# Rotary tables, head norm weights, lambda vectors and most parameters of a transformer layer loaded after the last modulation chunk instead of before it

## The chip, the core and the metric

The kernel runs on one core of one Trainium2 chip. The metric is the device time in microseconds of one execution; of several runs the median counts. Five engines work side by side, each in its own fixed order: TensorE (PE in the profile, with PEld for its weight loads), VectorE (DVE), ScalarE (ACT), GpSimd (POOL) and SyncE (SP), which here only issues DMA transfers. An instruction waits until the semaphores it names have reached a value, and everything behind it on its engine waits with it.

## What is computed

One layer of a diffusion transformer on 256 latent tokens `x` and 256 context tokens, model width 2048. The part that the change touches is at the front: modulation columns, the normalised and modulated hidden tokens, and q and k with a norm over each head, a rotary turn by table, and a difference of two softmaxes weighted by lambda.

```python
lam = (jnp.exp(jnp.sum(lambda_q1[l] * lambda_k1[l]))
       - jnp.exp(jnp.sum(lambda_q2[l] * lambda_k2[l])) + lam_init)
mod = (jax.nn.silu(c) @ w_mod[l] + b_mod[l])[:, None, :]
sa, ca, ga, sm, cm, gm = jnp.split(mod, 6, axis=-1)
h = modulate(x, norm_attn_w[l], sa, ca)          # rmsnorm(x, w) * (1 + ca) + sa
p = h @ w_in[l]
q = axial_rope(rmsnorm(split_qk(p[..., Q_OFF:K_OFF]), q_norm_w[l]), row, col)
k = axial_rope(rmsnorm(split_qk(p[..., K_OFF:V_OFF]), k_norm_w[l]), row, col)
mix = token_mixer(q, k_all, v_all, ..., lam, lam_init, subln_w[l], pool_w[l], pool_scale[l], ...)
x = x + ga * mix
x = x + gm * sq_relu_mlp(modulate(x, norm_mlp_w[l], sm, cm), w_ff1[l], w_ff2[l])
```

`k_all` and `v_all` hold latent and context tokens; the context runs through the same norm, weights and a modulation of its own.

## The kernel before

**Tiling.** Weights stream from memory in chunks of 128 x 1024 fp32 (512 KB), issued by SP. A product is done in three matmuls on split operands: ACT copies the chunk's high part (`whi`), DVE subtracts it to get the low part (`wlo`). Both have three buffers, so a new `whi` waits until PE is done with the one three chunks back.

**Modulation stage.** The loop `for f in range(KT)` runs over 16 feature tiles. For each it loads four chunks of `w_m` (`mod_tile`, PE groups `mod`), turns the result (`blocks` on DVE, `modT` on PE) into columns (`col`), and makes 128 hidden features of both token sets (`features`: `hw`, `hL`, `hC` on DVE and ACT). Beside it the first halves of k (`w_k` banks: k0, k1 for latent tokens, k2, k3 for context) and q (`w_q` banks: q0, q1) are accumulated feature by feature (`product`), one chunk of `w_k` or `w_q` per tile. In this loop the order of PE, ACT and DVE is that of the code (`ordered`, `pin`).

**Parameters.** One tile `prm` of 128 x 325 holds the identity `ident` for transposes, `c`, biases, norm weights, pool scales, edge factors and the small matrix `stack`; SP loads it first of all, ahead of `xT` (L298). Rotary tables, head norm weights and lambda vectors lie in `in_prq` (640 columns); POOL issues their loads (L207), as entries `prq` of the load list behind the first `w_m` chunk of tiles 9 and 11. POOL has nothing else to do there, so the scheduler lets the first three go at the kernel's start and the fourth (`lq2`, `lk2`, into the same buffer) as soon as the first lambda sum is done. `tables(0)`, `tables(1)` and `tables(2)` follow the features of tiles 9, 11 and 13: the cosine and sine tables times the q norm weight (with 1/8), times the k norm weight, and lambda.

**Evacuation stage.** Behind the loop come `qk_evac` for k0 to k3, then q0 and q1. ACT copies a bank to `qraw` and squares it to `qsq`; DVE sums (`qss`), takes the root with ACT's logarithm and exponential (`rsq`: `rq_y`, `rq_t`), scales, and for k0, k1, q0, q1 multiplies by two tables; POOL adds both products; PE turns the result with `ident` (`qkT`), ACT copies it to `kT` or `qT`. The transposes are due a fixed number of weight chunks later (`later`, `tick`: 3, 4, 5, 6 chunks for k0 to k3, 6 and 7 for q0 and q1), while PE works on the eight chunks of `w_v`, part 0 (`v`). Working tiles (`work`) share nine buffers of 2 KB. Here the scheduler orders ACT and DVE. DVE also accumulates the gate modulation (`ga_bc`, L648 and L650) from chunks that are loaded and due between the others.

The instructions of the modulation loop all show line 68 in the profile (the `pin` helper).

Of the kernel before, what the change touches and what calls it, by code (L numbers as in the profile page):

```python
# [23 lines left out]
LAM0 = 0.8 - 0.6 * math.exp(0.0)
# [3 lines left out]
WINDOWS = (2, 4, 8, 16)  # L28


PRM = {}
_o = 0
for _n, _w in (("ident", 128), ("c", 16), ("cc", 16), ("bca", 16), ("bsa", 16), ("nw", 16), ("nmw", 16),
               ("pscale", 8), ("subln", 1), ("edge", 60), ("stack", 32)):
    PRM[_n] = (_o, _o + _w)
    _o += _w
PRM_W = _o

PRQ = {}
_o = 0  # L40
for _n, _w in (("cos", 128), ("sin", 128), ("wk", 64), ("wq", 64), ("lq1", 64), ("lk1", 64),
               ("lq2", 64), ("lk2", 64)):
    PRQ[_n] = (_o, _o + _w)
    _o += _w
# [4 lines left out]
def layer(ctx: ExitStack, tc, a, out):  # L49
    nc = tc.nc  # L50
# [4 lines left out]
    pin = tc.keep_in_program_order  # L55
# [19 lines left out]
    def work(name, shape=None, dt=F32):  # L75
        return pool.tile(shape or [P, 512], dt, tag="w2", name=name, bufs=9)
# [51 lines left out]
    def plan(name, *idx, rate=0.0):  # L128
        stream.append(((name,) + idx, rate))
# [3 lines left out]
    for f in range(KT):  # L133
        for i in range(4):
            plan("w_m", f, i)
            if i == 0 and f in (9, 11):
                plan("prq", f // 2 - 4)
        if f == 0:
            for i in range(4):
                plan("cT", i)  # L140
        if f % 2 == 0:
            plan("w_k", 0, f // 2)
        if f % 2 == 1 and f > 1 or f == 0:
            plan("w_q", 0, f // 2)
# [55 lines left out]
    def load_next():  # L200
        key, rate = stream[len(loaded)]
        src = a[key[0]]
        for i in key[1:] if key[0] != "prq" else ():
            src = src[i]
        if key[0] == "prq":
            for dst, names in prq[key[1]]:
                nc.gpsimd.dma_start(dst, a["prq"][:, PRQ[names[0]][0]:PRQ[names[-1]][1]])  # L207
            loaded.append((key, None, None))
            return
        if key[0] in ("cT", "x"):  # L210
            dst = cT[:, 4 * key[1]:4 * key[1] + 4, :] if key[0] == "cT" else x1_tile()[:, key[1], key[2] * 512:key[2] * 512 + 512]
            nc.sync.dma_start(dst, src)
            loaded.append((key, None, None))
            return
        n = src.shape[-1]
        if key[0] == "w_m":
            raw = mod_raw(*key[1:])
            sp.dma_start(raw, src)
            loaded.append((key, raw, raw))
            return  # L220
        if key[0] in ("w_k", "w_q") and key[1] == 0:
            raw = pool.tile([P, n], F32, tag="aT", name="raw", bufs=2)
            sp.dma_start(raw, src)
            loaded.append((key, raw, raw))
            return
        raw = raw_chunk(src, n)
        if key[:3] == ("w_ff2", 7, 3):
            r3 = raw.rearrange("p (k f) -> p k f", k=2)
            vec.tensor_mul(r3, r3, mods["gm"][:, 1536:2048].unsqueeze(1).broadcast_to([P, 2, 512]))
        if key == ("w_ff1a", 0):  # L230
            hi, lo = (pool.tile([P, n], F32R, tag="aT", name=nm, bufs=2) for nm in ("hi0", "lo0"))
        elif key == ("w_o", 3, 4):
            pair = s8("pair", [P, 2, 1024], F32R)
            hi, lo = pair[:, 0, :], pair[:, 1, :]
        elif key in (("w_ff1a", 2), ("w_ff1a", 3)):
            i = 2 * (key[1] - 2)
            if i == 0:
                early.append(s16("early", [P, 4, 1024], F32R))
            hi, lo = early[0][:, i, :], early[0][:, i + 1, :]
        elif key == ("w_ff1a", 1):  # L240
            halves = [[work(nm, dt=F32R) for nm in ("hi1", "lo1")] for _ in range(2)]
            for h in range(2):
                split(*halves[h], raw[:, h * 512:h * 512 + 512])
            loaded.append((key, *zip(*halves)))
            return
        else:
            hi = pool.tile([P, n], F32R, tag="whi", name="whi", bufs=3)
            lo = pool.tile([P, n], F32R, tag="wlo", name="wlo", bufs=3)
        act.copy(hi, raw)  # L249
# [44 lines left out]
        return y  # L294


    prm = pool.tile([P, PRM_W], F32, tag="prm", name="prm")
    nc.sync.dma_start(prm, a["prm"])  # L298
    xT = s16("xT", [P, KT, T])
    cT = s16("cT", [P, KT, T])  # L300
    for i in range(4):
# [32 lines left out]
    wkt = pool.tile([P, 64], F32, tag="wkt", name="wkt")
    wqt = pool.tile([P, 3, 64], F32, tag="wqt", name="wqt")
    prq = (((tabs[:, 2:4], ("cos", "sin")), (wkt, ("wk",)), (wqt, ("wq", "lq1", "lk1"))),
           ((wqt[:, 1:3], ("lq2", "lk2")),))
    lam2 = pool.tile([P, 2], F32, tag="lam2", name="lam2")
    nlam = lam2[:, 0:1]

    sub8 = pool.tile([P, 1], F32, tag="sub8", name="sub8")
    vec.tensor_scalar(sub8, pr("subln"), 1.0 - LAM0, None, ALU.mult)

    def lam_sum(i):
        lm = work("lm", [P, 64])
        vec.tensor_mul(lm, wqt[:, 1, :], wqt[:, 2, :])
        vec.reduce_sum(lam2[:, i:i + 1], lm, axis=AX.X)

    def tables(part):

        if part == 0:
            lam_sum(0)
            vec.tensor_scalar(wqt[:, 0, :], wqt[:, 0, :], 0.125, None, ALU.mult)
        if part < 2:
            wv = wkt if part else wqt[:, 0, :]
            for t in range(2):
                vec.tensor_mul(tabs[:, 2 * part, t, :], tabs[:, 2, t, :], wv)
                so = tabs[:, 2 * part + 1, t, :].rearrange("p (a b f) -> p a b f", a=2, b=2)
                si = tabs[:, 3, t, :].rearrange("p (a b f) -> p a b f", a=2, b=2)
                wr = wv.rearrange("p (a b f) -> p a b f", a=2, b=2)  # L360
                for b in range(2):
                    vec.tensor_mul(so[:, :, b, :], si[:, :, b, :], wr[:, :, 1 - b, :])
            return
        lam_sum(1)
        act.activation(lam2, lam2, AF.Exp)
        vec.tensor_sub(nlam, lam2[:, 1:2], nlam)
        vec.tensor_scalar(nlam, nlam, -LAM0, None, ALU.add)
# [191 lines left out]
    for f in range(KT):  # L559
# [28 lines left out]
        if f == KT - 1:  # L588
            product("kx", f - 1)
            features(f)  # L590
        if f % 2 == 1:
            keep("w_q", f // 2, first_chunk("w_q", 0, f // 2))
        for n in ("kx", "kc", "q") if 2 < f < KT - 1 else ("kc", "q") if f == 2 else ("kc",):
# [2 lines left out]
            keep("w_k", f // 2, first_chunk("w_k", 0, f // 2))  # L596
        if f < KT - 1:
            features(f)
        if f in (9, 11, 13):
            tables(f // 2 - 4)  # L600
    for n, k in (("kx", KT - 1), ("kc", KT - 1), ("q", KT - 2), ("q", KT - 1)):
        product(n, k)
    while len(loaded) < FIRST_LOADS + 2:
        load_next()
    ordered_pe[0] = ordered[0] = False
    kb, qb = fb["w_k"], fb["w_q"]
    qT = s8("qT", [P, NH, T])
# [212 lines left out]
    def pool_diff(g, w, ps, sums):  # L820

        d = work("d")
        n0, n1 = w // 2, w // 2 - 1
        e0 = PRM["edge"][0] + sum(x - 1 for x in WINDOWS[:g]) * 2
        for i, s in enumerate(sums):
            pin(vec.tensor_mul(s[:, 0:n0], s[:, 0:n0], prm[:, e0:e0 + n0]))
            if n1:
                pin(vec.tensor_mul(s[:, T - n1:T], s[:, T - n1:T], prm[:, e0 + n0:e0 + n0 + n1]))
            sl = slice(i * T, i * T + T)
            pin(vec.scalar_tensor_tensor(d[:, sl], s, 1.0 / w, ps[:, sl], ALU.mult, ALU.subtract))  # L830
        diff.append((work("dh", dt=F32R), work("dl", dt=F32R)))
        later(1, partial(split, *diff[-1], d))
# [380 lines left out]
```

## Time and profile before

| | |
|---|---|
| median of 3 runs | 1448.89 us (1448.64 to 1449.95) |
| profiled execution, its own time | 1449.65 us |
| its span, first to last instruction | 1447.9 us |
| mean granted clock of PE | 0.997 |
| VectorE busy | 984.4 us (68%) |
| ScalarE busy | 674.5 us (47%) |
| moved by DMA | 355.23 MB, mean 245 GB/s |

A page of the profile lists the busy time of each engine, the span in 40 slices, the DMA queues, the chain of work that ended last, and the costliest groups of instructions. Views of the trace give the rest: who waited for whom, the instructions of an engine in order of time, DMA issues with the time to landing, and busy time by windows. In a timeline row stand the start, the duration, the engine, the line, the operation, what it writes and reads, shapes, and in brackets how long the engine had been idle and what ended that. Consecutive equal instructions are one row, with their count.

### The profile page before, as it was taken

To read this page: it belongs to the slowest core of one execution; us is meant where nothing else is said; L and a number is where in the kernel's file an instruction comes from. 1 tells how busy PE (TensorE), PEld (TensorE's weight loads), DVE (VectorE), ACT (ScalarE), POOL (GpSimd) and SP (SyncE) were. 2 spreads that over 40 slices of the span, in tenths; PEclk is the share of its full clock that TensorE was granted. 3 is DMA by queue.
4 is the path that set the end of the run, shared out by engine and by line. 5 is a ranking of instruction groups with operands and counts; after the bars stand their busy time and mean duration, and the time that the engine had idled before them with its cause. 6 is when DMAs were issued, how large, how long until landed. Compare 5 with 4: busy or idle time off the path is not lost.

```text
span 1447.9 us, 19760 instructions
## 1 busy us (share of the span) xinstructions
PE 1430.3 (99%) x7448; PEld 1178.6 (81%) x7448; DVE 984.4 (68%) x1226; ACT 674.5 (47%) x901; POOL 171.4 (12%) x188
## 2 busy tenths in 40 slices
PE   6999999999999999999999999999999999999998
PEld 4667887788888888888878888888888888888887
DVE  4568785768888777787766665656657555555676
ACT  5235336466644444444535545445354453544432
POOL 1001110001520111110101100011000110000260
PEclk9999999999999999999999999999999999999999
DMA  9996683335699999999746776777766665565553
GB/s 378 409 407 249 216 315 118 97 127 168 194 304 323 357 325 338 333 357 334 226 160 208 239 242 229 252 231 255 251 228 241 216 204 189 190 201 187 191 195 127
DMA packets 100976, 355.23 MB, mean 245 GB/s; under 512 B 12864, under 2 KB 13520, under 8 KB 100880
## 3 DMA queue, kind: packets, MB, share of 16 engines
q1 hardware_dynamic: 96336, 344.93, 68.6%
q0 software_dynamic: 4256, 8.77, 2.7%
q8 instruction: 58, 0.95, 0.3%
q14 instruction: 38, 0.31, 0.1%
q10 hardware_dynamic: 288, 0.26, 0.1%
HBM read 347.61 MB, written 2.17 MB: 242 GB/s over the span
## 4 chain that ended last, share of the span: by engine, by line
PE 93%; DMA 5%; DVE 1%; ACT 0%; issue 0%; SPq 0%; DVEq 0%
PE f L1060 14%; PE f L460 8%; PE f L459 8%; PE f L465 8%; PE f L1062 7%; DMA raw<-in_w_m_dram 4%; PE pg L459 4%; PE pg L460 4%; PE pg L465 4%; PE pyy L460 2%; PE pyy L459 2%; PE v L460 2%; PE pyy L465 2%; PE v L459 2%; PE v L465 2%; PE wo L460 2%
## 5 line engine op out<-in xcount | busy, mean ns | idle before, releaser
L250 DVE TENSOR_TENSOR wlo<-raw,whi 128x1024 fp32r<-128x1024 f32 x428 | 527.7, 1243 | 288.5 <-ACT whi L249 190.9
L249 ACT CAST whi<-raw 128x1024 fp32r<-128x1024 f32 x428 | 447.9, 1047 | 513.5 <-PE f L460 184.0
L1060 PE MATMUL f<-h,whi 128*128 128x512 f32 x896 | 213.9, 391 | 0.0
L460 PE MATMUL f<-whi,act 128*128 128x512 f32 x512 | 199.4, 389 | 0.0
L459 PE MATMUL f<-whi,act 128*128 128x512 f32 x512 | 199.3, 389 | 0.0
L1060 PEld LDWEIGHTS f<-h,whi 128*128 128x128 f32 x896 | 165.1, 188 | 32.1
L465 PE MATMUL f<-wlo,act 128*128 128x512 f32 x512 | 136.9, 389 | 0.0
L1062 PEld LDWEIGHTS f<-h,wlo 128*128 128x128 f32 x896 | 114.9, 191 | 4.4
L1062 PE MATMUL f<-h,wlo 128*128 128x256 f32 x896 | 116.2, 283 | 0.0
L465 PEld LDWEIGHTS f<-wlo,act 128*128 128x128 f32 x512 | 96.1, 188 | 19.9
L460 PEld LDWEIGHTS f<-whi,act 128*128 128x128 f32 x512 | 96.2, 188 | 19.7
L459 PEld LDWEIGHTS f<-whi,act 128*128 128x128 f32 x512 | 96.2, 188 | 19.7
L459 PE MATMUL pg<-whi,hL 128*128 128x512 f32 x256 | 100.3, 392 | 0.0
L460 PE MATMUL pg<-whi,hL 128*128 128x512 f32 x256 | 99.7, 389 | 0.0
L1070 POOL TENSOR_TENSOR rsq<-relu 128x512 f32<-128x512 f32 x28 | 29.1, 1038 | 457.7 <-ACT relu L1069 447.5
L650 DVE SCALAR_TENSOR_TENSOR sb<-raw,sil,sb 128x1024 f32<-128x1024 f32 x60 | 76.8, 1280 | 0.0
L465 PE MATMUL pg<-wlo,hL 128*128 128x512 f32 x256 | 68.5, 389 | 0.0
L465 PEld LDWEIGHTS pg<-wlo,hL 128*128 128x128 f32 x256 | 48.1, 188 | 10.1
L459 PEld LDWEIGHTS pg<-whi,hL 128*128 128x128 f32 x256 | 48.1, 188 | 9.9
L460 PEld LDWEIGHTS pg<-whi,hL 128*128 128x128 f32 x256 | 48.1, 188 | 9.9
L277 DVE TENSOR_TENSOR act<-rsq,act 128x512 fp32r<-128x512 f32 x28 | 19.3, 690 | 53.3 <-ACT act L276 53.3
L1084 DVE TENSOR_TENSOR acc<-f,acc 128x512 f32<-128x512 f32 x48 | 30.9, 686 | 20.5 <-PE f L465 20.5
(288 smaller groups left out, 2189.5 us busy)
## 6 DMA issues: line engine op xcount, KB each, us to landing
raw<-in_w_ff_dram SPq DMA_DIRECT2D x240, 512.0 KB, 4.3
raw<-in_w_m_dram SPq DMA_DIRECT2D x64, 512.0 KB, 10.2
raw<-in_w_ga_dram SPq DMA_DIRECT2D x32, 512.0 KB, 4.2
raw<-in_w_gb_in_dram SPq DMA_DIRECT2D x32, 512.0 KB, 5.1
raw<-in_w_cm_dram SPq DMA_DIRECT2D x32, 512.0 KB, 5.6
raw<-in_w_ga_in_dram SPq DMA_DIRECT2D x32, 512.0 KB, 5.7
raw<-in_w_sm_dram SPq DMA_DIRECT2D x32, 512.0 KB, 5.6
raw<-in_w_o_dram SPq DMA_DIRECT2D x32, 512.0 KB, 5.4
```

The costliest lines, as they stand in the source:

```text
L249: act.copy(hi, raw)
L250: vec.tensor_sub(lo, raw, hi.bitcast(F32))
L277: vec.tensor_sub(lo, src, hi.bitcast(F32))
L459: pe.matmul(banks[t], tok(h, k, 0, tt), wt, start=k == 0, stop=False)
L460: pe.matmul(banks[t], tok(h, k, 1, tt), wt, start=False, stop=False)
L465: pe.matmul(banks[t], tok(h, k, 0, tt), wt, start=False, stop=k == 2 * nk - 1)
L650: pin(vec.scalar_tensor_tensor(o, raw, sil[:, 0, k:k + 1], o, ALU.mult, ALU.add))
L1060: pe.matmul(ps, hi[:, kk * P:kk * P + P], both(h2, k), start=k == 0, stop=False)
L1062: pe.matmul(ps[:, T:2 * T], los[k // 8][:, k % 8 * P:k % 8 * P + P], act_slice(h2, k, 0), start=False, stop=k == KT - 1)
L1070: gp.tensor_mul(sq, r, r)
L1084: vec.tensor_add(acc[:, t, gs], bs[t], acc[:, t, gs])
```

## The change

The layout of `prm` is changed so that what the start needs (112 of 325 columns) comes first; the other 213, with `ident`, `nmw`, `pscale`, `subln` and `edge`, go to a tile `prm_late`. The entries `prq` are gone from the load list. A new function `late_loads`, called right behind the features of tile 15, writes one column of each of four tiles on DVE and then has POOL load them: `wqk` (both head norm weights), `tabs` (cosine and sine), `prm_late`, and `lamv` (the four lambda vectors, in one of the nine working buffers). The write makes each load wait for that place. `tables(1)` now stands behind the loop, ahead of the k evacuations; `tables(0)` and `tables(2)` stand between the evacuations of k and of q, in the order of the code. `tables(0)` now overwrites the cosine and sine tiles.

```diff
-for _n, _w in (("ident", 128), ("c", 16), ("cc", 16), ("bca", 16), ("bsa", 16), ("nw", 16), ("nmw", 16),
-               ("pscale", 8), ("subln", 1), ("edge", 60), ("stack", 32)):
+for _n, _w in (("c", 16), ("cc", 16), ("bca", 16), ("bsa", 16), ("nw", 16), ("stack", 32), ("ident", 128), ("nmw", 16),
+               ("pscale", 8), ("subln", 1), ("edge", 60)):
...
+PRM_1 = PRM["ident"][0]
...
-            if i == 0 and f in (9, 11):
-                plan("prq", f // 2 - 4)
...
-        if key[0] == "prq":
-            for dst, names in prq[key[1]]:
-                nc.gpsimd.dma_start(dst, a["prq"][:, PRQ[names[0]][0]:PRQ[names[-1]][1]])
-            loaded.append((key, None, None))
-            return
...
-    prm = pool.tile([P, PRM_W], F32, tag="prm", name="prm")
-    nc.sync.dma_start(prm, a["prm"])
+    prm = pool.tile([P, PRM_1], F32, tag="prm", name="prm")
+    nc.sync.dma_start(prm, a["prm"][:, 0:PRM_1])
+    prm_late = pool.tile([P, PRM_W - PRM_1], F32, tag="prm_late", name="prm_late")
...
-    vec.tensor_scalar(sub8, pr("subln"), 1.0 - LAM0, None, ALU.mult)
+
+    def late_loads():
+
+        lamv.append(work("lamv", [P, 4, 64]))
+        for dst, src in ((wqk, a["prq"][:, PRQ["wq"][0]:PRQ["wk"][1]]), (tabs[:, 0:2], a["prq"][:, 0:PRQ["sin"][1]]),
+                         (prm_late, a["prm"][:, PRM_1:PRM_W]),
+                         (lamv[0], a["prq"][:, PRQ["lq1"][0]:PRQ["lk2"][1]])):
+            flat = dst if len(dst.shape) == 2 else dst[:, 0, :] if len(dst.shape) == 3 else dst[:, 0, 0, :]
+            vec.memset(flat[:, 0:1], 0.0)
+            nc.gpsimd.dma_start(dst, src)
...
-        lam_sum(1)
+        vec.tensor_scalar(sub8, pr("subln"), 1.0 - LAM0, None, ALU.mult)
+        for i in range(2):
+            lam_sum(i)
         act.activation(lam2, lam2, AF.Exp)
...
         if f == KT - 1:
             product("kx", f - 1)
             features(f)
+            late_loads()
...
-        if f in (9, 11, 13):
-            tables(f // 2 - 4)
...
     while len(loaded) < FIRST_LOADS + 2:
         load_next()
+    tables(1)
...
     for t in range(4):
         qk_evac(kb[t], t, 0, kT, 2, 3 + t)
+    ordered[0] = True
+    tables(0)
+    tables(2)
+    ordered[0] = False
     for t in range(2):
         qk_evac(qb[t], t, 0, qT, 0, 6 + t)
```

The order of PE and of SP is the same in both programs. On POOL the four loads of `in_prq` ahead of and behind the eight rows of biases (`row`) are gone, and the four late loads stand behind them.

On DVE, at the end of the modulation loop (from `hw` of tile 15 on), there stood:

```order
L68 SCALAR_TENSOR_TENSOR hw<-xT,col,rms 128x256
L68 SCALAR_TENSOR_TENSOR hw<-cT,col,rms 128x256
L68 SCALAR_TENSOR_TENSOR hL_727<-hw,col,hL_727 128x256
L68 SCALAR_TENSOR_TENSOR hC_728<-hw,col,hC_728 128x256
L68 TENSOR_TENSOR wlo<-raw,whi 128x1024 x3
L477 TENSOR_REDUCE qss<-qsq 128x8
```

Now there stands, from the last two rows of the features on:

```order
L69 SCALAR_TENSOR_TENSOR hL_725<-hw,col,hL_725 128x256
L69 SCALAR_TENSOR_TENSOR hC_726<-hw,col,hC_726 128x256
L69 MEMSET wqk 128x1
L69 MEMSET tabs 128x1
L69 MEMSET prm_late 128x1
L69 MEMSET lamv 128x1
L69 TENSOR_TENSOR wlo<-raw,whi 128x1024 x3
L69 TENSOR_TENSOR tabs<-tabs,wqk 128x64
L69 TENSOR_TENSOR tabs<-tabs,wqk 128x2x16 x2
L69 TENSOR_TENSOR tabs<-tabs,wqk 128x64
L69 TENSOR_TENSOR tabs<-tabs,wqk 128x2x16 x2
L481 TENSOR_REDUCE qss<-qsq 128x8
```

The six products of `tables(1)`, which need two of the loads, have come between the last `wlo` of the loop and the first sum for k0.

Further down on DVE, around the last table product for q0 (`qraw_1313<-qraw_1313,tabs_86`; q1 is `qraw_1333`), there stood:

```order
L650 SCALAR_TENSOR_TENSOR ga_bc_1353<-raw_1429,sil_80,ga_bc_1353 128x1024
L480 TENSOR_TENSOR qraw_1313<-qraw_1313,rq_y_1319 128x512
L292 SCALAR_TENSOR_TENSOR rq_t_1342<-qss_1337,rq_t_1342 128x8
L250 TENSOR_TENSOR wlo_1465<-raw_1462,whi_1464 128x1024
L487 TENSOR_TENSOR qsq_1315<-qraw_1313,tabs_86 128x8x16 x4
L293 SCALAR_TENSOR_TENSOR rq_y_1339<-rq_t_1342,rq_y_1339 128x8
L650 SCALAR_TENSOR_TENSOR ga_bc_1353<-raw_1468,sil_80,ga_bc_1353 128x1024
L489 TENSOR_TENSOR qraw_1313<-qraw_1313,tabs_86 128x512
L480 TENSOR_TENSOR qraw_1333<-qraw_1333,rq_y_1339 128x512
L487 TENSOR_TENSOR qsq_1335<-qraw_1333,tabs_86 128x8x16 x4
L250 TENSOR_TENSOR wlo_1504<-raw_1501,whi_1503 128x1024
```

Now q0 is `qraw_1318` and q1 `qraw_1338`:

```order
L244 TENSOR_TENSOR wlo_1509<-raw_1506,whi_1508 128x1024
L287 SCALAR_TENSOR_TENSOR rq_y_1324<-rq_t_1327,rq_y_1324 128x8
L285 SCALAR_TENSOR_TENSOR rq_t_1347<-rq_y_1344 128x8
L658 SCALAR_TENSOR_TENSOR ga_bc_1358<-raw_1512,sil_81,ga_bc_1358 128x1024
L484 TENSOR_TENSOR qraw_1318<-qraw_1318,rq_y_1324 128x512
L286 SCALAR_TENSOR_TENSOR rq_t_1347<-qss_1342,rq_t_1347 128x8
L491 TENSOR_TENSOR qsq_1320<-qraw_1318,tabs_87 128x8x16 x4
L287 SCALAR_TENSOR_TENSOR rq_y_1344<-rq_t_1347,rq_y_1344 128x8
L493 TENSOR_TENSOR qraw_1318<-qraw_1318,tabs_87 128x512
L484 TENSOR_TENSOR qraw_1338<-qraw_1338,rq_y_1344 128x512
L491 TENSOR_TENSOR qsq_1340<-qraw_1338,tabs_87 128x8x16 x4
L244 TENSOR_TENSOR wlo_1548<-raw_1545,whi_1547 128x1024
```

The `wlo` of the seventh `w_v` chunk (`wlo_1504` before, `wlo_1509` now) and the `ga_bc` step of its neighbour stand ahead of q0's last product now, where they stood behind it.

On ACT, around q0's root (`rq_y_1319` before: logarithm, then exponential):

```order
L249 CAST whi_1425<-raw_1423 128x1024
L288 ACTIVATE rq_y_1319<-qss_1317,epsb_73 128x8
L498 COPY kT_1242<-qkT_1431 128x4x128
L289 ACTIVATE rq_y_1319<-rq_y_1319,ebias_71 128x8
L288 ACTIVATE rq_y_1339<-qss_1337,epsb_73 128x8
L289 ACTIVATE rq_y_1339<-rq_y_1339,ebias_71 128x8
L249 CAST whi_1464<-raw_1462 128x1024
```

And now (`rq_y_1324`):

```order
L477 COPY qraw_1318<-w_q_0_242 128x512
L479 ACTIVATE qsq_1320<-w_q_0_242 128x512
L477 COPY qraw_1338<-w_q_1_243 128x512
L479 ACTIVATE qsq_1340<-w_q_1_243 128x512
L69 ACTIVATE lam2_89<-lam2_89 128x2
L282 ACTIVATE rq_y_1324<-qss_1322,epsb_74 128x8
L243 CAST whi_1508<-raw_1506 128x1024
L283 ACTIVATE rq_y_1324<-rq_y_1324,ebias_72 128x8
L282 ACTIVATE rq_y_1344<-qss_1342,epsb_74 128x8
```

Between the two halves of q0's root stands the `whi` cast of the seventh `w_v` chunk instead of a copy of `kT`, and lambda's exponential has come ahead of them.

More of the change, by code (lines that the diff above doesn't have):

```diff
@@ L37 @@
 PRM_W = _o
+PRM_1 = PRM["ident"][0]
 PRQ = {}
 _o = 0
-for _n, _w in (("cos", 128), ("sin", 128), ("wk", 64), ("wq", 64), ("lq1", 64), ("lk1", 64),
+for _n, _w in (("cos", 128), ("sin", 128), ("wq", 64), ("wk", 64), ("lq1", 64), ("lk1", 64),
                ("lq2", 64), ("lk2", 64)):
@@ L202, in load_next @@
         src = a[key[0]]
-        for i in key[1:] if key[0] != "prq" else ():
+        for i in key[1:]:
             src = src[i]
-        if key[0] == "prq":
-            for dst, names in prq[key[1]]:
-                nc.gpsimd.dma_start(dst, a["prq"][:, PRQ[names[0]][0]:PRQ[names[-1]][1]])
-            loaded.append((key, None, None))
-            return
         if key[0] in ("cT", "x"):
@@ L305, in pr @@
         lo, hi = PRM[name]
-        return prm[:, lo:hi]
+        return prm[:, lo:hi] if hi <= PRM_1 else prm_late[:, lo - PRM_1:hi - PRM_1]
     ident = pr("ident")
@@ L333, in layer @@
     tabs = pool.tile([P, 4, 2, 64], F32, tag="tabs", name="tabs")
[L334 to L337, printed above, removed]
+    wqk = pool.tile([P, 2, 64], F32, tag="wqk", name="wqk")
+    wkt = wqk[:, 1, :]
+    lamv = []
     lam2 = pool.tile([P, 2], F32, tag="lam2", name="lam2")
@@ L341, in layer @@
     sub8 = pool.tile([P, 1], F32, tag="sub8", name="sub8")
-    vec.tensor_scalar(sub8, pr("subln"), 1.0 - LAM0, None, ALU.mult)
+    def late_loads():
[6 more added lines that the diff above has]
+            nc.gpsimd.dma_start(dst, src)
     def lam_sum(i):
         lm = work("lm", [P, 64])
-        vec.tensor_mul(lm, wqt[:, 1, :], wqt[:, 2, :])
+        vec.tensor_mul(lm, lamv[0][:, 2 * i, :], lamv[0][:, 2 * i + 1, :])
         vec.reduce_sum(lam2[:, i:i + 1], lm, axis=AX.X)
     def tables(part):
-        if part == 0:
-            lam_sum(0)
-            vec.tensor_scalar(wqt[:, 0, :], wqt[:, 0, :], 0.125, None, ALU.mult)
         if part < 2:
-            wv = wkt if part else wqt[:, 0, :]
+            wv = wqk[:, part, :]
+            if part == 0:
+                vec.tensor_scalar(wv, wv, 0.125, None, ALU.mult)
             for t in range(2):
-                vec.tensor_mul(tabs[:, 2 * part, t, :], tabs[:, 2, t, :], wv)
+                vec.tensor_mul(tabs[:, 2 * part, t, :], tabs[:, 0, t, :], wv)
                 so = tabs[:, 2 * part + 1, t, :].rearrange("p (a b f) -> p a b f", a=2, b=2)
-                si = tabs[:, 3, t, :].rearrange("p (a b f) -> p a b f", a=2, b=2)
+                si = tabs[:, 1, t, :].rearrange("p (a b f) -> p a b f", a=2, b=2)
                 wr = wv.rearrange("p (a b f) -> p a b f", a=2, b=2)
@@ L823, in pool_diff @@
         n0, n1 = w // 2, w // 2 - 1
-        e0 = PRM["edge"][0] + sum(x - 1 for x in WINDOWS[:g]) * 2
+        e0 = sum(x - 1 for x in WINDOWS[:g]) * 2
         for i, s in enumerate(sums):
-            pin(vec.tensor_mul(s[:, 0:n0], s[:, 0:n0], prm[:, e0:e0 + n0]))
+            pin(vec.tensor_mul(s[:, 0:n0], s[:, 0:n0], pr("edge")[:, e0:e0 + n0]))
             if n1:
-                pin(vec.tensor_mul(s[:, T - n1:T], s[:, T - n1:T], prm[:, e0 + n0:e0 + n0 + n1]))
+                pin(vec.tensor_mul(s[:, T - n1:T], s[:, T - n1:T], pr("edge")[:, e0 + n0:e0 + n0 + n1]))
             sl = slice(i * T, i * T + T)
```

## The prediction

> **What bounds the kernel now.** The page comes first: busy times by engine.
>
> ```profile
> span 1447.9 us, 19760 instructions
> ## 1 busy us (share of the span) xinstructions
> PE 1430.3 (99%) x7448; PEld 1178.6 (81%) x7448; DVE 984.4 (68%) x1226; ACT 674.5 (47%) x901; POOL 171.4 (12%) x188
> ```
>
> TensorE (PE) is idle for 1447.9 - 1430.3 = 17.6 us in all, so nothing can be won but part of that, and every new wait of PE is lost time unless a later wait swallows it. The waits view of PE says where the idle time is, first for 0 to 130 us, then for the rest (columns: total us, times, longest).
>
> ```profile
> PE ssq L68 <- DVE sq L68: 9.4, 2, 7.7
> PE w_k L68 <- ACT hL L68: 1.6, 1, 1.6
> PE mod L68 <- DMA raw<-in_w_m_dram: 0.8, 3, 0.4
> ```
>
> ```profile
> PE qkT L497 <- ACT e L718: 0.5, 1, 0.5
> PE pd L281 <- DVE dl L277: 0.5, 1, 0.5
> ```
>
> Almost all of it lies in the first 35 us. Behind 130 us only 1.0 us is left, so a stall there has next to nothing to disappear into. The windows view gives the stages (columns: length, busy us and instructions of PE, PEld, DVE, ACT, POOL, then granted clock, DMA share, GB/s).
>
> ```profile
> 40.00:60.00 20.00, 20.00 (x197) 13.39 (x199) 11.60 (x26) 5.55 (x9) 0.00 (x0) 1.00 1.03 408
> ...
> 120.00:140.00 20.00, 19.99 (x96) 15.85 (x95) 17.29 (x39) 14.35 (x28) 2.77 (x2) 1.00 0.58 202
> 140.00:160.00 20.00, 20.00 (x97) 16.63 (x96) 19.96 (x34) 6.77 (x12) 6.00 (x3) 1.00 0.55 175
> ```
>
> Two stages matter. In the modulation stage (to about 120 us, one stretch of it is shown) the DMA queues are full (share 1.03, 408 GB/s) and PE is full too, while VectorE (DVE) has eight us in twenty to spare. From 120 to 160 us it is the reverse: the queues are half empty and DVE is full, 19.96 us of 20. The change takes bytes and DVE work out of the first stage and puts both into the second.
>
> **What the first stage gains.** Removed ahead of the last modulation chunk are 213 columns of `prm` (213 x 128 x 4 = 0.109 MB) and the 640 columns loaded from `in_prq` (0.328 MB). At 408 GB/s the 0.437 MB are worth 1.07 us. Small rows cost more than their bytes. The DMA view of 0 to 20 us, and then that of 84 to 96 us for the last of these loads, give the share of the 16 engines that the POOL queue took:
>
> ```profile
> q0 software_dynamic: 384, 0.30, 5.0%
> ```
>
> ```profile
> q0 software_dynamic: 32, 0.07, 1.5%
> ```
>
> 5.0% of 20 us is 1.0 us, 1.5% of 12 us is 0.18 us, and `prm` is 0.109/408 = 0.27 us: 1.45 us is the upper end. That PE gets all of it isn't given, since PE is itself gapless from 40 us on. PE wins by two ways: `xT` lands earlier, so the first squares and all that hangs on them move up, and its three waits for `w_m`, 0.8 us together, shrink. I put the first way at the 0.26 + 0.11 MB that left the queues before the last `xT`, 0.37/0.408 = 0.9 us, less some share that PE doesn't pass on. Ends: 0.6 and 1.45; I take **1.1 us gained**, the value of the plain bytes. The DVE work taken out there (20 table, lambda and `sub8` instructions) wins nothing: DVE waits for PE in every step of that stage.
>
> **What the second stage pays.** Now follow DVE. Its timeline before, around the end of the last features:
>
> ```profile
> 122.73 0.48 DVE L68 SCALAR_TENSOR_TENSOR hC<-hw,col,hC 128x256 fp32r<-128x256 f32 x1
> 123.67 3.50 DVE L68 TENSOR_TENSOR wlo<-raw,whi 128x1024 fp32r<-128x1024 f32 x3 [0.45 <-ACT whi L68]
> 127.08 0.68 DVE L477 TENSOR_REDUCE qss<-qsq 128x8 f32<-128x512 f32 x1
> 128.86 0.17 DVE L291 SCALAR_TENSOR_TENSOR rq_t<-rq_y 128x8 f32<-128x8 f32 x1 [1.10 <-ACT rq_y L289]
> ```
>
> From 127.08 to 160 us the only idle time is the 1.10 us shown. The POOL additions for k0, k1 and q0 (the rotary sums), and of the transposes on PE that take their results those for k0 and q0, are these:
>
> ```profile
> 133.00 2.20 POOL L490 TENSOR_TENSOR qraw<-qraw,qsq 128x512 f32<-128x512 f32 x1 [44.92 <-DVE rq_t L292]
> 139.43 1.65 POOL L490 TENSOR_TENSOR qraw<-qraw,qsq 128x512 f32<-128x512 f32 x1 [4.22 <-DVE qraw L489]
> 152.11 1.61 POOL L490 TENSOR_TENSOR qraw<-qraw,qsq 128x512 f32<-128x512 f32 x1 [11.04 <-DVE qraw L489]
> ```
>
> ```profile
> 138.90 0.60 PE L497 MATMUL qkT<-prm,qraw 128*128 128x128 f32 x4
> ...
> 156.61 1.04 PE L497 MATMUL qkT<-prm,qraw 128*128 128x128 f32 x8
> ```
>
> The x8 are four for k3 and four for q0. q0's begin about 1.04 - 0.60 = 0.44 us in, near 157.05 us, and its sum was there at 152.11 + 1.61 = 153.72 us: **3.3 us of slack**. k0's was there at 135.20 for 138.90: 3.7 us. PE's order is unchanged, so these are the places where it would wait.
>
> Step 1, the late loads. The four memsets stand behind hC, end 123.21 us, where DVE idled 0.45 us before `wlo`, and a memset of that size took 0.06 us in the run's first us (the first row below), so they are free. They release the loads on POOL. What such a load took, from the DMA view (KB, us from issue to landing), between the longest and the shortest POOL transfer:
>
> ```profile
> 0.82 0.06 DVE L312 MEMSET epsb<- 128x1 f32 x1
> ```
>
> ```profile
> ga_bc<-row POOLq DMA_DIRECT2D x2, 512.0 KB, 7.8
> ...
> tabs<-in_prq_dram POOLq DMA_DIRECT2D x1, 128.0 KB, 5.2
> ...
> gm_bc<-gm_bc POOLq DMA_DIRECT2D x2, 32.0 KB, 3.1
> ```
>
> `wqk` is issued at 123.3, `tabs` some 0.55 us later, at 123.85. With 5.2 us, the row of the same tile, `tabs` lands at 129.05; the bounds are 126.95 and 131.65. `tables(1)` waits for it, and in DVE's order everything of the k and q evacuations stands behind it, as do the low parts of the next `w_v` chunks. DVE was free at 127.08, so it starts **1.97 us late** (0 to 4.6). POOL holds nothing behind the loads but the k0 sum; the parameters with `ident` land two issues later, near 130.2, long before the transposes at 138.90.
>
> Step 2, work that comes ahead of q0's sum on DVE. The pieces, as they ran before:
>
> ```profile
> 87.00 0.22 DVE L68 TENSOR_TENSOR lm<-wqt 128x64 f32<-128x64 f32 x1
> 87.25 0.22 DVE L68 TENSOR_REDUCE lam<-lm 128x1 f32<-128x64 f32 x1
> 87.39 0.18 DVE L68 TENSOR_SCALAR wqt<-wqt 128x64 f32<-128x64 f32 x1
> 87.60 0.77 DVE L68 TENSOR_TENSOR tabs<-tabs,wqt 128x64 f32<-128x64 f32 x6
> 88.29 0.44 DVE L68 STREAM_TRANSPOSE blocks<-mod 128x256 f32<-128x256 f32 x1
> ```
>
> ```profile
> 156.14 1.27 DVE L650 SCALAR_TENSOR_TENSOR ga_bc<-raw,sil,ga_bc 128x1024 f32<-128x1024 f32 x1
> ```
>
> From start to start, six table products hold DVE 0.69 us (87.60 to 88.29), with the scaling 0.90; a lambda sum 0.39 (87.00 to 87.39). So: `tables(1)` 0.69, `tables(0)` 0.90, two lambda sums and the two operations that end lambda 1.0, `sub8` 0.1. And by the order one more `wlo` (three took from 123.67 to 127.08, 1.1 each) and one more `ga_bc` (1.27, 1.2 with the same overlap) now stand ahead of q0's last product, five and four where there were four and three. Together **5.0 us**.
>
> Step 3, a new wait of DVE. On ScalarE q0's logarithm and exponential now have a `whi` cast between them, as the ACT rows show; before, q0's root was ready when DVE came for it.
>
> ```profile
> 149.09 1.05 ACT L249 CAST whi<-raw 128x1024 fp32r<-128x1024 f32 x1 [2.69 <-PE v L460]
> ```
>
> The same pair, with a shorter square between, made DVE wait 1.10 us for k0 (above). With 1.05 us between, and 0.3 us of lambda operations for DVE to do meanwhile, I take **1.3 us**; the ends are 0, if other rows fill it, and 1.10 + 1.05 = 2.15.
>
> Sum for q0: 1.97 + 5.0 + 1.3 = 8.3 us later against 3.3 us of slack, a stall of **5.0 us** on PE near 157 us. The gain doesn't reduce it: PE and DVE both come 1.1 us earlier. With the landing at its late bound it is 7.6, with step 3 at its upper end too 8.5; with the early bound and without step 3 it is 5.0 - 3.3 = 1.7. For k0, ahead of its sum stand 1.97, 0.69 and one `wlo` more, 3.9 us against 3.7 of slack: next to no stall, and one in the late case. q1, whose transposes come a whole weight chunk behind q0's, gains the length of the stall and stays covered. Step 4 is the clock.
>
> ```profile
> 15.00:20.00 5.00, 2.40 (x28) 0.99 (x20) 3.84 (x9) 2.94 (x7) 0.00 (x0) 0.97 1.03 415
> 20.00:25.00 5.00, 5.00 (x16) 3.92 (x16) 3.68 (x6) 4.54 (x7) 0.00 (x0) 0.69 1.03 409
> ```
>
> PE idled 2.6 us of five, and its clock was lowered behind that: (0.03 + 0.31) x 5 = 1.7 us of full-speed time lost. A stall of 5 us should bring this on again, part of it while PE is still idle: **1.2 us** (0 to 1.7). The Trainium skill, "TensorE: Matmul & The Clock Gate", Part 1, says that the clock is halved after an idle window of about 3.4 us, in windows that run freely. This trace shows it after 2.6 us in pieces already, so 5 us should do by either.
>
> **The sum.** -1.1 + 5.0 + 1.2 = +5.1 us. On the profiled execution's 1449.65 us that is 1454.75; that execution lies 0.76 us over the median of the runs, 1448.89, so a median of **1454.0 us** is forecast, 0.35% slower. Bounds, from the median: -1.45 + 1.7 + 0 gives 1449.1; -0.6 + 8.5 + 1.7 gives 1458.5.
>
> **The rivals.**
> - *The stall doesn't come.* If the loads land before 126.95 us and DVE gets at q0's rows without the new wait, 5.0 us of work meets 3.3 us of slack, and another 1.7 us found (in DVE's 1.10 us of idle time and in its waits for the POOL sums, which fall elsewhere in the new order) hides all. Left is the gain: 1447.8 us. It decides when DVE's delay falls under 3.3 us. For it speaks that DVE has just 17.29 us of work from 120 to 140; against it, the 19.96 of the next 20 and the fixed order. Chance 0.16.
> - *The loads land early,* in 3.1 us like the quickest POOL row, so that `tables(1)` never waits: the stall is 1.97 us shorter, 1448.89 - 1.1 + 3.0 + 1.2 = 1452.0. For it: the queues are emptying when the loads are issued, and were full for the 5.2 us; against it: most POOL rows are nearer to 5 us than to 3. Chance 0.12. The Trainium skill, "DMA: Bandwidth & Descriptors", section "Anatomy of one DMA — SWDGE (gpsimd) path", speaks for this one: it fits such a load as 2.0 us plus bytes over 436 GB/s, an estimate of 2.3 us for `tabs`, where the row has 5.2.
> - *The loads land late,* 7.8 us after issue: k0's transpose stalls too and the PE total is 7.6: 1448.89 - 1.1 + 7.6 + 1.2 = 1456.6. For it: four loads are issued in a row; against it: the queues are half empty there. Chance 0.08.
> - *No stall, and the start loses its low-clock stretch,* because PE's early gaps move: -1.1 - 1.7 gives 1446.1. Chance 0.06.
>
> That the loads aren't held back at all isn't likely: POOL's rows wait for DVE.
>
> **How the numbers follow.** The forecast itself has 0.58. A measurement of this kernel can tell about 0.2%, 2.9 us, from no change. Of the 0.58, 0.04 lies under 1451.8 (no lowered clock, step 3 filled), of the early landing half, 0.06. So slower 0.54 + 0.06 + 0.08 = 0.68, within 0.2% 0.04 + 0.06 + 0.16 = 0.26, faster 0.06. The range is that of the bounds, 1449.1 to 1458.5; what it leaves out is the case without any stall, 0.16, and the one with the better start, most of whose 0.06 is under it.
>
> **What would show it.** In the profile after: PE's waits should have a row of `qkT` waiting for POOL's `qraw`, near 5 us in one piece, and no other new row; DVE should idle some 2 us ahead of the first `tabs` products; the waits for `w_m` should shrink from 0.8 us and the last `mod` matmuls come about 1.1 us earlier; the granted clock should dip in the stretch behind 160 us. It is wrong if `tabs` lands within 3 us of issue, if q0's transposes start without a wait, or if the `mod` matmuls end no earlier.

## The result, and the profile after

| | before | after |
|---|---|---|
| median | 1450.13 us, 12 runs | 1453.14 us, 12 runs |
| profiled execution, its own time | 1449.65 us | 1453.45 us |
| its span | 1447.9 us | 1451.6 us |

The changed kernel takes 1.0018 times as long, with a 95% interval of 1.001 to 1.0026: 2.6 us, from 1.5 to 3.8. One of the 12 runs of before took 1782.6 us; it is in the median but not in the ratio, and without it the median of before is 1449.95 us. The medians of the table lie 3.0 us apart. Note that the median of before lies 1.2 us over that of the three runs the prediction started from.

The page of the changed kernel, its first lines: PE is idle for 1451.6 - 1432.1 = 19.5 us, 1.9 more than before, while its busy time grew by 1.8, though it does the same 7448 matmuls. So the loss has two halves: waits, and matmuls that ran slower.

```profile
span 1451.6 us, 19767 instructions
...
PE 1432.1 (99%) x7448; PEld 1179.4 (81%) x7448; DVE 982.9 (68%) x1230; ACT 675.7 (47%) x901; POOL 170.0 (12%) x188
```

PE's waits after (total us, times, longest). New are the second row, the wait for q0's sum, and the fourth; the row for `w_m` is gone.

```profile
PE ssq L69 <- DVE sq L69: 8.4, 2, 6.7
PE qkT L501 <- POOL qraw L494: 2.8, 1, 2.8
PE w_k L69 <- ACT hL L69: 1.6, 1, 1.6
PE pg L463 <- ACT whi L243: 1.0, 1, 1.0
```

The timeline of PE after, at the first `w_v` matmul and at the transposes of k3 and q0. Before, `v` began at 128.01 and the transposes of k3 at 156.61: PE comes to both 1.9 us earlier, and then gives back 2.79 us in one piece.

```profile
126.04 0.39 PE L463 MATMUL v<-whi,hL 128*128 128x512 f32 x1
...
154.71 0.60 PE L501 MATMUL qkT<-prm_late,qraw 128*128 128x128 f32 x4
158.10 1.11 PE L501 MATMUL qkT<-prm_late,qraw 128*128 128x128 f32 x4 [2.79 <-POOL qraw L494]
```

The windows of that place (length, busy us of PE, PEld, DVE, ACT, POOL, granted clock, DMA share, GB/s). The clock falls to 0.78 and 0.88: (0.22 + 0.12) x 5 = 1.7 us of full-speed time. DVE, 19.96 of 20 before, is at 18.61 in the 20 us.

```profile
140.00:160.00 20.00, 17.21 (x81) 14.15 (x80) 18.61 (x47) 8.46 (x16) 1.89 (x2) 0.94 0.56 184
155.00:160.00 5.00, 2.21 (x10) 1.77 (x9) 4.96 (x12) 1.17 (x2) 1.58 (x1) 0.78 0.41 146
160.00:165.00 5.00, 5.00 (x21) 4.07 (x20) 1.73 (x2) 1.05 (x1) 2.17 (x1) 0.88 0.67 195
```

Upstream, DVE's timeline after shows the three things that came in ahead of q0: a wait for the table load, the tables and lambda, and a new wait for ScalarE at 150.74.

```profile
125.92 0.77 DVE L69 TENSOR_TENSOR tabs<-tabs,wqk 128x64 f32<-128x64 f32 x6 [0.70 <-DMA tabs<-in_prq_dram]
126.60 0.68 DVE L481 TENSOR_REDUCE qss<-qsq 128x8 f32<-128x512 f32 x1
128.32 0.17 DVE L285 SCALAR_TENSOR_TENSOR rq_t<-rq_y 128x8 f32<-128x8 f32 x1 [1.04 <-ACT rq_y L283]
...
139.07 1.27 DVE L285 SCALAR_TENSOR_TENSOR rq_t<-rq_y 128x8 f32<-128x8 f32 x1
...
144.73 0.19 DVE L69 TENSOR_SCALAR wqk<-wqk 128x64 f32<-128x64 f32 x1
144.95 0.77 DVE L69 TENSOR_TENSOR tabs<-tabs,wqk 128x64 f32<-128x64 f32 x6
...
150.74 0.17 DVE L285 SCALAR_TENSOR_TENSOR rq_t<-rq_y 128x8 f32<-128x8 f32 x1 [1.25 <-ACT rq_y L283]
...
155.63 0.69 DVE L493 TENSOR_TENSOR qraw<-qraw,tabs 128x512 f32<-128x512 f32 x1
```

POOL's sums for k0, k1 and q0 after. q0's ends at 156.47 + 1.58 = 158.05, where the transposes start. In relation to the start of `v` on PE that is 32.0 us; before it was 153.72 - 128.01 = 25.7. The sum is 6.3 us later, against the 3.3 us of slack.

```profile
133.49 1.28 POOL L494 TENSOR_TENSOR qraw<-qraw,qsq 128x512 f32<-128x512 f32 x1 [9.73 <-DVE rq_t L286]
138.72 1.59 POOL L494 TENSOR_TENSOR qraw<-qraw,qsq 128x512 f32<-128x512 f32 x1 [3.95 <-DVE qraw L493]
156.47 1.58 POOL L494 TENSOR_TENSOR qraw<-qraw,qsq 128x512 f32<-128x512 f32 x1 [16.15 <-DVE qraw L493]
```

The DMA view of 110 to 135 us after (KB, us from issue to landing): the late loads took 3.3 to 3.9 us.

```profile
tabs<-in_prq_dram POOLq DMA_DIRECT2D x1, 128.0 KB, 3.6
lamv<-in_prq_dram POOLq DMA_DIRECT2D x1, 128.0 KB, 3.3
prm_late<-in_prm_dram POOLq DMA_DIRECT2D x1, 106.5 KB, 3.4
wqk<-in_prq_dram POOLq DMA_DIRECT2D x1, 64.0 KB, 3.9
```

### The profile page after: what moved, and what is told of

It reads as the page before. It is cut to its first block, busy times and chain, and to the rows that moved or that the text cites. A ratio compares the mean times of both kernels' runs of the same rounds, so it can differ in the third digit from the quotient of the medians.

```text
span 1451.6 us, 19767 instructions
## 1 busy us (share of the span) xinstructions
PE 1432.1 (99%) x7448; PEld 1179.4 (81%) x7448; DVE 982.9 (68%) x1230; ACT 675.7 (47%) x901; POOL 170.0 (12%) x188
## 4 chain that ended last, share of the span: by engine, by line
PE 87%; issue 8%; DVE 2%; DMA 2%; ACT 1%; POOL 0%; DVEq 0%; ACTq 0%; POOLq 0%
PE f L1068 14%; PE f L464 8%; PE f L463 8%; PE f L469 8%; PE f L1070 7%; PE pg L463 4%; PE pg L464 4%; PE pg L469 4%; PE wo L463 2%; PE pyy L463 2%; PE pyy L464 2%; PE wo L469 2%; PE wo L464 2%; PE pyy L469 2%; PE v L463 1%
```

## The experiments

Theory: all that the change loses, it loses at q0's transposes, since DVE's rows ahead of q0's sum grew; the early loads it takes away are a gain. Rivals: the work has to be paid in any place; part of the loss lies elsewhere (a weight chunk near 505 us); the late landing or the late `ident` sets it. All edits are to the changed kernel unless said otherwise.

**Later q turns (e1).** The sums stay as late as they are; PE just doesn't ask for them yet.

```diff
-        qk_evac(qb[t], t, 0, qT, 0, 6 + t)
+        qk_evac(qb[t], t, 0, qT, 0, 7 + t)
```

> The transposes of q0 and q1 on PE stand one weight chunk later; DVE's order is that of the changed kernel. Theory A (the loss is PE's one wait for q0's POOL sum, 2.79 us, and the 1.7 us of lowered clock behind it): no wait of qkT for qraw, clock 1.00 from 155 to 165 us, and only the 1.9 us gained by 126 us is left: 1448.2 us where before has 1450.1, ratio 0.9987. Rival B (the work added to DVE between 125 and 160 us has to be paid, so the wait only moves, to the low parts of w_v or to q1): at least 1 us of PE waits in another row between 155 and 200 us, ratio 1.000 or over. Rival C (the 1.3 us that PE lost at a weight chunk near 505 us belong to the change too): no wait for qraw, but 0.9996, with a wait of pg for whi near 500 us.

Measured: 1448.81 us beside 1449.75 of before, ratio 0.999 (0.9981 to 0.9999). PE has no wait for `qraw`. Its windows show no idle time and a full clock where the changed kernel lost both, and DVE is as full as there:

```profile
155.00:160.00 5.00, 5.00 (x26) 4.12 (x25) 4.96 (x14) 1.15 (x2) 1.61 (x1) 1.00 0.49 179
160.00:165.00 5.00, 5.00 (x26) 4.12 (x25) 5.00 (x5) 1.08 (x2) 3.31 (x1) 1.00 0.58 179
```

The same work on DVE, in the same order, costs nothing once PE's demand stands one chunk later, so B falls. Between this kernel and the changed one lie 1.0018 - 0.999 = 0.0028, 4.1 us, about the 2.8 of the wait and the 1.7 of the clock. This version is faster than the changed kernel, and faster than before by a margin that the interval only just separates from nothing. The interval doesn't exclude C's 0.9996; the second profile of the changed kernel (below) answers C.

**Lambda behind q (e2).** The rows of lambda and `sub8` go behind q1's product; PE's order is unchanged.

```diff
     tables(0)
-    tables(2)
     ordered[0] = False
     for t in range(2):
         qk_evac(qb[t], t, 0, qT, 0, 6 + t)
+    ordered[0] = True
+    tables(2)
+    ordered[0] = False
```

> The lambda rows and sub8 stand behind q1's last product on DVE; the tables stay ahead of q0. Theory A (DVE rows ahead of q0's sum pass to PE one for one): 1.0 us of rows and the wlo that ran among them, 1.2, no longer stand there, so q0's sum is 2.2 us earlier in relation to PE, the wait for qraw falls from 2.79 to about 0.6 us, and there is no lowered clock behind it: ratio 0.9991. Rival B (these rows filled DVE's waits for ScalarE, which now grow by as much): the wait stays over 2 us, clock dip as before, ratio 1.0015 or over.

Measured: ratio 0.9991 (0.9983 to 1.0); no wait for `qraw`, clock 1.00. The effect was larger than forecast. POOL's row for q0, and PE's transposes of k3 and q0:

```profile
151.19 1.82 POOL L494 TENSOR_TENSOR qraw<-qraw,qsq 128x512 f32<-128x512 f32 x1 [10.58 <-DVE qraw L493]
```

```profile
154.85 1.04 PE L501 MATMUL qkT<-prm_late,qraw 128*128 128x128 f32 x8
```

`v` starts at 126.19 here, so the sum ends 153.01 - 126.19 = 26.8 us behind it, 5.2 us earlier than in the changed kernel (I had reckoned with 2.2). Gone from ahead of q0 are the lambda rows (some 0.9), the wait of 1.25, one `wlo` (1.1) and two `ga_bc` (1.2 each), 5.6 in all; one row of q1 (0.6) came in. The lambda rows themselves are a sixth of it: the rest is what their fixed place let in or held up. This edit moves more than those rows, though: ScalarE copies q0's bank at 132.16 us here, at 143.97 in the changed kernel and at 129.87 before. Why the changed kernel has that copy so late isn't shown. One rival is untested: each lambda sum takes one of the nine working buffers ahead of q0. `lamv`, which holds another, isn't the reason, since here it is read until 157 us and the wait is gone all the same.

**Loads one chunk earlier (e3).** `late_loads()` behind the features of tile 14 instead of 15.

```diff
             features(f)
-            late_loads()
...
+        late_loads() if f == KT - 2 else None
```

> The four late loads are issued one modulation chunk earlier; the orders of PE, ScalarE and POOL are those of the changed kernel, on DVE only the four memsets move. Theory A (the landing adds to the stall what DVE waits for it, 0.70 us): DVE doesn't wait ahead of the first tabs products, the wait of qkT for qraw falls from 2.79 to 2.1 us, the clock dip gets shorter by little: ratio 1.0012. Rival B (the landing is absorbed, since DVE waits later for ScalarE anyway): the wait stays at 2.8. Rival C (0.4 MB come back into full queues and cost the modulation stage): PE starts v later than 126.04 us by up to 1 us.

Measured: ratio 1.0021 (1.0013 to 1.003), not told apart from the changed kernel's 1.0018. DVE's timeline has no wait ahead of the tables, but a longer one for ScalarE two rows later, 1.40 us instead of 1.04:

```profile
125.79 0.76 DVE L69 TENSOR_TENSOR tabs<-tabs,wqk 128x64 f32<-128x64 f32 x6
...
128.55 0.17 DVE L285 SCALAR_TENSOR_TENSOR rq_t<-rq_y 128x8 f32<-128x8 f32 x1 [1.40 <-ACT rq_y L283]
```

```profile
PE qkT L501 <- POOL qraw L494: 2.4, 1, 2.4
```

So half of the 0.70 us is absorbed and 0.4 reaches PE: A and B each have half. C isn't settled: `v` starts at 126.70 us, 0.7 later than in the changed kernel's first profile, but its kin with the loads in the old place reach 126.78. In the full queues (DMA share 1.02 to 1.04 from 115 to 124 us) the same loads took longer, `tabs` 5.4 us:

```profile
tabs<-in_prq_dram POOLq DMA_DIRECT2D x1, 128.0 KB, 5.4
```

**Parameters alone (e4), tables alone (e5).** e4 is the kernel before with `prm` loaded in two parts; e5 is the changed kernel with `prm` loaded whole at the start. First e4's edit, then e5's.

```diff
...
-    nc.sync.dma_start(prm, a["prm"])
+    nc.sync.dma_start(prm, a["prm"][:, 0:PRM_1])
...
+    def late_loads():
+        vec.memset(prm_late[:, 0:1], 0.0)
+        nc.gpsimd.dma_start(prm_late, a["prm"][:, PRM_1:PRM_W])
...
+            late_loads()
```

> From the kernel before: only the parameters are loaded in two parts, the larger one behind the last modulation chunk; rotary and lambda work stays in the modulation stage (sub8 is made behind q1). Theory A (plain bytes: 0.109 of 0.437 MB): gain 0.3 to 0.5 us by 126 us, no wait of qkT for qraw, ratio 0.9997. Rival B (the head of the queue counts: PE's first matmul came 1.0 us earlier in the changed kernel, since the first load is short): first matmul near 6.7 us, gain 1 us or more by 126 us, ratio 0.9992. Rival C (the start's lowered clock decides the gain, and shifts by chance): gain by 126 us other than the gain at the first matmul by over 0.5 us.

```diff
...
-    nc.sync.dma_start(prm, a["prm"][:, 0:PRM_1])
+    nc.sync.dma_start(prm, a["prm"])
...
-                         (prm_late, a["prm"][:, PRM_1:PRM_W]),
```

> The changed kernel, but with the parameters loaded whole at the start as before; rotary and lambda work late. Theory A (the early gain comes from both parts by their bytes, 0.328 of 0.437 MB here, and the loss from DVE's order alone): first matmul of PE between 6.71 and 7.72 us, v starts 0.8 to 1.3 us earlier than before, PE waits 2.6 to 3.0 us for q0's qraw with the clock dip behind it: ratio 1.0025. Rival B (the parameters make the gain): v starts within 0.4 us of before, ratio 1.003. Rival C (the late parameters, behind which the transposes wait for ident, are part of the loss): the wait for qraw falls under 2 us.

Measured: e4 0.9997 (0.9988 to 1.0005), no wait for `qraw`; e5 1.0024 (1.0015 to 1.0033). `v` starts at 127.01 in e4 and at 126.60 in e5, both ahead of every profile of before (127.69 to 128.70, below), so each part seems to gain by itself, and all of the loss comes with the tables. Against the mean of before the gains are 1.1 and 1.5 us, more than I expected of either (0.3 to 0.5, 0.8 to 1.3) and 2.6 together, where the whole change gains 1.7: one profile each doesn't divide the gain. That the parameters with `ident` come late has no share in it (rival C of e5 falls). In e5's profile the wait is there but the clock, against my expectation, stayed full behind it:

```profile
PE qkT L498 <- POOL qraw L491: 2.9, 1, 2.9
```

```profile
155.00:160.00 5.00, 2.11 (x14) 1.66 (x13) 4.96 (x14) 1.17 (x2) 1.58 (x1) 1.00 0.50 184
160.00:165.00 5.00, 5.00 (x26) 4.11 (x25) 2.41 (x4) 1.05 (x1) 2.18 (x1) 1.00 0.58 165
```

That execution took 1451.61 us, the shortest of the 11 of e5, whose median is 1453.72.

**Loads later (e6).** The loads are issued behind the three `wlo` rows, just ahead of `tables(1)`.

```diff
-            late_loads()
...
-    tables(1)
+    late_loads(); tables(1)
```

> The late loads are issued 4 us later, behind the three wlo on DVE instead of ahead of them, so the landing is waited for: one qss sum runs ahead of it, DVE's wait for tabs grows from 0.70 to about 3.4 us. Theory A (what DVE starts late passes to PE at q0 one for one, beyond the slack already used up): the wait of qkT for qraw grows from 2.79 to 5 us or more, the clock dip behind it is longer than 1.7 us of full-speed time, ratio 1.0040 or over. Rival B (DVE's later waits for ScalarE, 1.04 and 1.25 us, take most of it, as they took half of 0.70 us when the loads came earlier): the wait grows by less than 1.2 us.

Measured: ratio 1.0045 (1.0032 to 1.0058). `tabs` landed 5.1 us after its issue, and DVE's row for the tables, PE's waits for `qraw` and the windows show what came of it:

```profile
132.00 0.81 DVE L69 TENSOR_TENSOR tabs<-tabs,wqk 128x64 f32<-128x64 f32 x6 [5.51 <-DMA tabs<-in_prq_dram]
```

```profile
PE qkT L501 <- POOL qraw L494: 5.8, 3, 4.4
```

```profile
160.00:165.00 5.00, 2.38 (x8) 2.09 (x9) 5.00 (x9) 0.59 (x1) 2.19 (x1) 0.62 0.44 142
165.00:170.00 5.00, 5.00 (x18) 3.96 (x17) 0.81 (x2) 0.98 (x1) 1.28 (x1) 0.70 0.33 105
```

DVE waited 4.8 us longer; one `qss` (0.7) ran ahead of the wait, and neither the 1.04 nor the 1.25 us wait for ScalarE is left. PE waited 5.8 us for `qraw`, 3.0 more than in the changed kernel: 4.4 for q0 and the rest for k0 and k1. The lowered clock comes to (0.38 + 0.30) x 5 = 3.4 us, some 0.7 of it while PE stood idle anyway. The delay passes to PE, though not one for one: A in its direction and in the ratio, B in that later waits take a part. DVE's and ScalarE's orders were planned anew here, so the split between them isn't exact.

**Both remedies (e7).** The edits of e1 and e2 together.

> Later q turns and the lambda rows behind q1's product together. Theory A (each alone takes PE's wait for qraw away, and nothing else was lost): no wait, no clock dip, the same time as either, ratio 0.9990. Rival B (a smaller wait was left in each that adds up, or the rows put behind now make the low parts of w_v late): other than 0.9990 by over 0.0005.

Measured: 1448.85 us beside 1450.09, ratio 0.999 (0.9981 to 0.9999), as e1 alone. Once PE doesn't wait, a smaller delay of DVE is worth nothing.

**Each kernel once more (e0, e9: before; e8: changed).** No edit; a second and third profile of before, and a second one of the changed kernel.

> The kernel before, profiled once more. Between 400 and 800 us PE lost 1.2 us more in the changed kernel than before, 0.4 in the one with later q turns, 1.4 and 1.2 in two others, at waits for weight chunks (whi); before's first profile has none there. Theory A (such waits come and go from execution to execution): this profile has some too, 0.3 us or more, and its span is other than 1447.9. Rival B (they come because PE is earlier against the weight stream): none here, as in the first profile.

> The kernel before, profiled a third time. Theory A: between 175 and 850 us PE differs from before's first profile by 0.3 us or more (the second differed by 0.10), since waits for weight chunks come and go. Rival B (the kernel before has none of them): within 0.15 us again.

> The changed kernel, profiled once more. Theory A (the wait at q0 belongs to the order of DVE, the rest of the profiled difference varies): the wait of qkT for qraw is 2.7 to 3.0 us again, v starts 1.2 to 2.0 us ahead of before's first profile, and what PE loses between 175 and 850 us against that profile is other than 1.22 us by 0.4 or more. Rival B (the 1.22 us is part of the change): 1.0 to 1.4 us again. The clock behind the wait may dip, as in two profiles with a wait of 2.4 to 2.8 us, or not, as in one with 2.9.

Measured: spans of 1447.6 and 1448.5 us for before and 1450.9 for the changed kernel. The waits of the second profile of the changed kernel have q0's again, and none of `pg` for `whi`:

```profile
PE qkT L501 <- POOL qraw L494: 2.8, 1, 2.8
```

The clock behind it dips as in the first, to 0.86 and 0.80, 1.7 us. Its PE lost nothing more against before between 175 and 850 us, where the first profile had lost 1.2. So the wait near 505 us is not part of the change; e3 had one of 1.1 us elsewhere (`pyy`). Against what I expected, e0 and e9 have none of these waits either: both are within 0.1 us of before's first profile. Why nine profiles of the changed kernel and its variants lost between none and 2.1 us there, and three of before next to none, stays open; the ratios of e1 and e7 leave little room for a lasting part.

The start of `v`, from the three profiles of before:

```profile
128.01 0.39 PE L459 MATMUL v<-whi,hL 128*128 128x512 f32 x1
```

```profile
127.69 0.39 PE L459 MATMUL v<-whi,hL 128*128 128x512 f32 x1
```

```profile
128.70 0.39 PE L459 MATMUL v<-whi,hL 128*128 128x512 f32 x1
```

Before thus begins `v` at 128.13 on the mean, with 1.0 us between executions (the third, like the second of the changed kernel, ran on another chip). The seven profiles that share the changed kernel's start (both of it, e1, e2, e6, e7, and e3, which differs only in when the loads are issued) lie between 126.04 and 126.78, mean 126.47: a gain of 1.7 us, and no overlap.

## Why the prediction was right, and where its sizes were off

The forecast was slower, by one wait at q0's transposes with a lowered clock behind it. That is what the runs show. 1454.0 us stands beside 1453.14, but the difference to before was forecast as 5.1 us and is 2.6; that the time came so close is owed in part to luck, the low median it started from. The 2.6 us are 0.18%, less than the 0.2% that the prediction thought could be told from no change; the interval does tell them from it.

| term | forecast | measured |
|---|---|---|
| gain up to `v` | -1.1 | -1.7 (seven profiles against three) |
| wait at q0 | 5.0 | 2.8 (both profiles) |
| lowered clock | 1.2 | 1.7 (both profiles; 0 in e5) |
| sum | +5.1 | +2.8; by the runs +2.6 |

*Gain.* Over my upper end of 1.45; the reason isn't shown. The ways I named for it don't hold up: the waits for `w_m`, 0 in the changed kernel's profile, are 1.2 in e1 with the same start, and 0.6 and 1.0 in the other profiles of before. The first matmul came at 7.72, 7.37 and 7.00 us before and at 6.71 and 6.97 after, but at 7.40 in e6 with the same start; a single pair of profiles would have told 1.0 us there.

*Step 1, the landing.* Mis-sized: I took 5.2 us from a load in full queues, and it was 3.6, near the early bound. DVE waited 0.70 us instead of 1.97. How full the queues are doesn't settle it: `tabs` took 5.4 us in e3's full queues, but also 5.1 in e6, where the DMA share over its way was 0.91, 0.90 and 0.36 (126 to 132 us in steps of two), against 0.98 and 0.90 for the 3.6 us (122 to 126). So emptying queues, the reason that the rival of early landing gave, don't explain it by themselves, and what sets the time stays open. That rival, with +3.1 us, was the nearest to the measured difference.

*Step 2, rows ahead of q0.* 5.0 forecast. Of the 6.3 us by which the sum is later, 0.8 are the landing (0.70, and 0.1 by which DVE ends `wlo` later in relation to PE) and 1.25 step 3, which leaves 4.2 (or 4.6, if only the 0.4 of e3 count for the landing). The list of rows was right. What I missed are stalls of DVE by POOL's sums, which lie otherwise in the new order (last section): 2.3 us before, 1.7 after, so 0.5 of the missing 0.8. Another 0.2 is that the lambda rows with `sub8` took 0.9 instead of 1.1.

*Step 3, the new wait.* 1.3 forecast, 1.25 measured. It wasn't taken away by itself: it went together with the lambda rows in e2.

*k0.* 134.77 us for transposes at 136.93: no stall, as forecast, and 2.2 us to spare where I had none.

*Step 4, the clock.* 1.7 us at a wait of 2.8, more than the 1.2 I gave to one of 5.0, and in one of four profiles with a wait of 2.4 to 2.9 us nothing. So it can come or not, and the runs bear that out: of e5's 11, the five with a mean granted clock of 0.998 took 1451.61 to 1454.23 us, the six with 0.995 or 0.996 took 1453.72 to 1455.78. The rival of a start without lowered clock is answered by before's third profile, which had none of it up to 35 us and still began `v` last of the three:

```profile
20.00:25.00 5.00, 4.38 (x17) 2.98 (x17) 3.91 (x6) 4.66 (x9) 0.00 (x0) 1.00 1.02 408
30.00:35.00 5.00, 3.40 (x24) 2.04 (x26) 2.44 (x7) 0.91 (x2) 0.00 (x0) 1.00 1.02 406
```

## What to carry to other kernels

When work moves into a stage, take the slack of each demand behind it, and look first whether the demand can move instead: one number here (the transposes one chunk later) turned 0.18% lost into 0.1% won, with the same work in the same place. Rows put into an engine's order by hand can cost more than they last, by what is let in ahead of the urgent rows and by the waits that come with it: here 0.9 us of rows went with 5.2 us of delay. One row isn't the price of a load: `tabs` took 3.6, 5.1, 5.2 and 5.4 us in four places, so carry both ends through the sum. And profile a kernel more than once before reading a difference of 1 us out of it.

## What the runs showed of the hardware beside this

A small DVE row that starts while POOL adds two tiles lasts until POOL is done. Two rows of before's DVE timeline, of a kind that takes 0.16 us elsewhere in it:

```profile
133.96 1.28 DVE L293 SCALAR_TENSOR_TENSOR rq_y<-rq_t,rq_y 128x8 f32<-128x8 f32 x1
...
139.80 1.30 DVE L292 SCALAR_TENSOR_TENSOR rq_t<-qss,rq_t 128x8 f32<-128x8 f32 x1
```

They end at 135.24 and 141.10, and the POOL sums quoted in the prediction at 135.20 and 141.08. After, the row at 139.07 (1.27) ends at 140.34, and POOL's at 140.31; beside it one product at 134.00, under POOL's sum for k0, took 1.32 us where its like take 0.69. Over the usual time that is 1.12 + 1.14 = 2.3 us of DVE before and 1.1 + 0.6 = 1.7 after. The Trainium skill, "SBUF — State Buffer", section "SBUF: two separate sides", has the rule: a DVE operation with two inputs from SBUF and a GpSimd one that reads it share a pair of ports, and whoever comes second is blocked for the whole instruction. These rows agree, and a forecast of DVE's time beside POOL should count it.

The clock was lowered after 2.4 to 2.8 us of waiting in three profiles, and not after 2.9 in another, so the length of a wait alone doesn't decide it. Windows of 1 us over the changed kernel's first profile show what the dip is: the granted clock stands at 0.50 for 3.41 us, from 157.78 to 161.19, which makes the 1.7.

```profile
157.00:158.00 1.00, 0.00 (x0) 0.00 (x0) 1.00 (x1) 0.00 (x0) 1.00 (x1) 0.89 0.33 131
158.00:159.00 1.00, 0.90 (x5) 0.90 (x5) 1.00 (x5) 0.00 (x0) 0.04 (x1) 0.50 0.09 37
```

Every dip up to 175 us in these profiles is of this kind, at 0.50 for 3.41 us, or for twice that in e6, and within one execution all of them start on one grid: at 17.83, 31.49 and 157.78 us here, 4 and 37 times 3.41 us apart. Laid over the wait at q0, the grid's stretch ahead of the dip held 2.48, 2.77 and 2.39 us of idle PE in the three profiles with a dip. In e5 the wait lies across a border of the grid, 1.90 us on one side and 0.99 on the other. That fits the missing dip, but one case doesn't show it, and in the first 35 us a stretch with 1.61 us idle was followed by a dip in before and by none in e5.
